# A hybrid decoder layer on one core: where the split weight operands lie in on-chip memory

## The chip, the core and the metric

The kernel runs on one core of one Trainium2 chip. The core has a matrix engine (TensorE, "PE" in the profile, with its weight loads as "PEld"), VectorE ("DVE"), ScalarE ("ACT"), GpSimd ("POOL") and SyncE ("SP"), whose queue issues most transfers. On-chip memory (SBUF) has 128 partitions; a tile takes the same range of bytes in each of them. The results of matmuls go to PSUM. The metric is the device time of one execution, in microseconds.

## The reference, cut to what matters

```python
def swiglu(u, w_in, w_out):
    gate, up = jnp.split(u @ w_in, 2, axis=-1)
    return (jax.nn.silu(gate) * up) @ w_out
...
        f1 = swiglu(rms_norm(h, ffn1_pre_g[l]), ffn1_w_in[l], ffn1_w_out[l])
        h = h + HALF_STEP * rms_norm(f1, ffn1_post_g[l])
        u = rms_norm(h, mix_pre_g[l])
        p_rwkv, p_swa, q_mem, gate_logits = _split(u @ w_in[l], IN_SIZES)
        y_a = rwkv7_mix(p_rwkv, ...)
        y_b = sliding_window_gqa_sinks(q_s, k_s, v_s, swa_sinks[l])
        y_c = memory_cross_attention(...)
        g_a, g_b, g_c = _split(jax.nn.sigmoid(gate_logits + gate_b[l]), (D, D, D))
        merged = (g_a * (y_a @ w_branch[l, 0]) + g_b * (y_b @ w_branch[l, 1])
                  + g_c * (y_c @ w_branch[l, 2]))
        h = h + rms_norm(merged @ w_out[l], mix_post_g[l])
        f2 = swiglu(rms_norm(h, ffn2_pre_g[l]), ffn2_w_in[l], ffn2_w_out[l])
        h = h + HALF_STEP * rms_norm(f2, ffn2_post_g[l])
```

There are 1024 tokens, a model width of 1024, an FFN width of 2816 and one layer; everything is float32. Nearly all of the arithmetic is in the products with the large weights: `w_in` and `w_out` of the two FFNs, `w_in` of the mixer, `w_branch` and `w_out`.

## The kernel before

Activations lie feature by feature: a tile has 128 features in the partitions and 512 tokens in the free dimension, and the tokens are worked in two halves of 512.

**A product in three matmuls.** A large product is made with float32 operands that are split in two float32r parts each: `hi` is the value rounded to float32r, `lo` is what is left. `mm3` (L314 to L319) then issues three matmuls into the same PSUM tile: `hi` weights with `hi` activations (L317), `hi` weights with `lo` activations (L318), and `lo` weights with `hi` activations (L319). Each matmul has 128 x 128 weights and 512 columns of the moving operand (256 in parts of the last stage), and each one loads its weights anew, the same `hi` block twice included. The weight load of a matmul runs while the matmul before it streams.

**How weights become operands.** A raw piece of weights, 128 partitions by four blocks of 128 columns (256 KB), is brought by SyncE's queue into one of five `w_raw` buffers (L246). `operand` (L251) makes `w_hi` from it with a ScalarE cast (L254) and `w_lo` with a VectorE subtraction (L256). Each side has eight buffers, which are used in turn (`OPS = 8`); `prefetch` keeps up to eight operands ahead of the matmuls. A cast therefore waits until the last matmul that reads the buffer's former content is done. For the FFN input products some sums and differences of raw weights are made first (L272 to L278, `w_sum`), and their results go through `operand` too. Eight operands of the last stage are kept in a pool of their own (`keep`), with tiles of the same names.

**Order.** The stages follow each other on TensorE: the first norm and the memory's keys and values; FFN 1 (input products, then output products in five chunks); the mixer's projections with the RWKV recurrence and the two attentions, between whose small matmuls the gates' projections are filled in; the branches and the output projection; FFN 2; and the last norm. The weights of all of them come through the same `operand` in one sequence, `self.seq`. Scheduling is left to a planner, with priorities around the casts (`high_priority`).

**Where the tiles lie.** All operand tiles, weights and activations, begin at a multiple of 32 bytes. A `w_hi` or `w_lo` tile is 4 x 128 numbers, 2048 bytes in each partition; block `k` is the contiguous piece of 512 bytes at `512 k`, and a matmul takes its weights from one such block: `tuple(t[:, k % 4] for t in w[k // 4])` (`block`) or `t[:, k]` (`product`).

Of the kernel before, what the change touches and what calls it, by code (L numbers as in the profile page):

```python
# [11 lines left out]
F32R = mybir.dt.float32r  # L12
# [5 lines left out]
P = 128  # L18
# [15 lines left out]
NPAIR = 4  # L34
MAIN_PSUM = ("po", "px", "py", "pr", "pgate", "pq", "pb", "pw")
OPS = 8
KEEP = 4
RAWS = 5
KH = KD // 2
# [161 lines left out]
class Builder:  # L201
# [4 lines left out]
    def plan(self):  # L206
        seq = []
        for f in ("ffn1", "ffn2"):
            items = [(f + "_gate", j) for j in range(FIRST[f])] + [(f + "_rest", j) for j in range(FIRST[f])]
            items += [(f + "_pair", j) for j in range(FIRST[f], KF)]  # L210
            items += [(f + "_out", q) for c in OUT_STRIPS for q in c]

            items += [(f + "_out", q) for q in OUT_STRIPS[-1]] * (f == "ffn1")
            if f == "ffn1":
                seq += items
                first = [("win", f) for f in MIX_FIRST]
                seq += first + [("win", f) for f in FILL] + first
                seq += [("win", f) for p in range(NPAIR) for f in (8 + p, 4 + p, p) if f not in MIX_FIRST]
                seq += [("win", j) for j in ATT_BLOCKS]
                seq += [("win", 24 + g) for g in range(24)]  # L220
                seq += [("wb", 4 * i + q) for i in BRANCHES + BRANCHES[2:] for q in range(4)]
                seq += [("wout", o) for o in range(KD)] * 2
            else:
                seq += items
        self.seq = seq
        self.raws = []
        for name, i in seq:
            f, _, kind = name.partition("_")
            if kind in ("gate", "rest", "pair"):
                self.raws += [(f + "_in", i)] + [(f + "_in", i + KF)] * (kind != "gate")  # L230
            else:
                self.raws.append((name, i))
        self.raw_pos, self.raw_ready = 0, []
        self.lead, self.urgent = 300, 1000
        self.op_base = self.op_use = self.op_pos = 0
        self.ops_ready = []
        self.gen = self.operands()

    def raw(self, ahead):
# [8 lines left out]
            self.raw_pos += 1  # L248
        return self.raw_ready.pop(0)

    def operand(self, x, pool=None):  # L251
        pool = pool or self.wpool
        hi = pool.tile([P, 4, P], F32R, tag="w_hi", name="w_hi", bufs=OPS)
        self.nc.scalar.copy(hi, x)  # L254
        lo = pool.tile([P, 4, P], F32R, tag="w_lo", name="w_lo", bufs=OPS)
        self.nc.vector.tensor_tensor(lo, x, hi.bitcast(F32), ALU.subtract)  # L256
        return hi, lo

    def operands(self):
        V = self.nc.vector  # L260
        for name, i in self.seq:
            kind = name.partition("_")[2]
            a1 = self.raw(RAWS - 1)
            a2 = self.raw(RAWS - 2)
            pool = self.keep if name == "ffn2_out" and i in OUT_STRIPS[-1][:KEEP] else None
            if kind != "rest":
# [14 lines left out]

    def prefetch(self, n=OPS, lead=None):
        with self.tc.high_priority(offset=self.lead if lead is None else lead):
            while self.op_pos < self.op_base + n:
                o = next(self.gen, None)
                if o is None:
                    return
                self.ops_ready.append(o)
                self.op_pos += 1
# [1066 lines left out]
    def build(self):  # L1356
        nc, tc, io = self.nc, self.tc, self.io
        with contextlib.ExitStack() as outer, tc.tile_pool(reuse_waits="tile", name="consts", bufs=1) as cp, \
# [44 lines left out]
            with quarters() as self.qpool:  # L1403
# [16 lines left out]
                with tc.tile_pool(reuse_waits="tile", name="ffn_out", bufs=2) as pool, \  # L1420
                     tc.tile_pool(reuse_waits="tile", name="keep", bufs=OPS) as self.keep:
                    acc = self.acc_tiles()
# [78 lines left out]
```

## Time and profile before

| | |
|---|---|
| median of the runs | 2378.95 us (2 runs, 2378.08 to 2379.82) |
| the profiled execution | 2381.53 us |
| its span, first to last instruction | 2379.8 us |
| mean granted TensorE clock | 0.996 |
| instructions | 33514 |
| moved by DMA | 323.80 MB, 136 GB/s over the span |

The profile is of one execution. "Busy" is the time in which an engine works on at least one instruction; matmuls are pipelined, so that the record of one matmul overlaps with the next, and their number times their duration is more than the busy time. In rows of groups the numbers behind the bar are busy us and the mean ns of one instruction, and behind the second bar the idle time before them with what ended it. In rows of the timeline the two numbers are the start and the duration in us; rows that follow each other on one engine without a gap may be merged, with their count behind an x.

### The profile page before, as it was taken

How to read it: one execution, taken by the hardware profiler on the slowest of the kernel's cores; microseconds unless marked ns; L12 is line 12 of the kernel's file. 1: busy time of each engine (PE TensorE's matmuls, PEld its weight loads, DVE VectorE, ACT ScalarE, POOL GpSimd, SP SyncE). 2: the span in 40 equal slices, each digit the busy share in tenths (PEclk: the TensorE clock that was granted, in tenths of full speed). 3: DMA queues.
4: the chain of work that ended last, by engine and by line, in shares of the span. 5: the costliest groups of instructions: out<-in, count | busy, mean ns of one | idle time of the engine just before them, and what ended most of it. 6: DMA issues, size and time to landing. Idle time of an engine off the chain costs nothing.

```text
span 2379.8 us, 33514 instructions
## 1 busy us (share of the span) xinstructions
PE 2343.9 (98%) x12388; PEld 1916.1 (81%) x12388; DVE 1543.4 (65%) x2584; ACT 891.6 (37%) x1648; POOL 95.5 (4%) x134
## 2 busy tenths in 40 slices
PE   8999999999999999999999999999999999999998
PEld 6788888888888777888868887778888888878888
DVE  6986555655478776894655456475998765564535
ACT  5423333422345444223454455234652233342211
POOL 0000000000000000001310000240000000000000
PEclk9999999999999999999999999999999999999999
DMA  7453222533244325325444324555545432263303
GB/s 277 136 188 121 86 87 80 178 115 106 97 161 142 110 99 189 135 93 175 144 156 153 123 97 150 185 188 166 174 162 183 156 120 82 83 202 100 114 23 107
DMA packets 196195, 323.80 MB, mean 136 GB/s; under 512 B 35360, under 2 KB 65568, under 8 KB 195776
## 3 DMA queue, kind: packets, MB, share of 16 engines
q1 hardware_dynamic: 180000, 294.33, 37.7%
q10 hardware_dynamic: 16032, 27.33, 3.4%
q8 instruction: 98, 1.61, 0.3%
q14 instruction: 65, 0.53, 0.1%
HBM read 231.41 MB, written 89.13 MB: 135 GB/s over the span
## 4 chain that ended last, share of the span: by engine, by line
PE 89%; DVE 5%; DMA 3%; ACT 2%; issue 1%; ACTq 0%; SPq 0%; DVEq 0%
PE po L317 7%; PE po L318 6%; PE po L319 6%; PE px L317 6%; PE px L318 6%; PE px L319 6%; PE pgate L317 4%; PE pgate L319 4%; PE pgate L318 4%; PE pz L317 3%; PE pz L318 3%; PE pz L319 3%; PE pr L319 2%; PE pr L317 2%; PE pr L318 2%; PE pb L318 2%
## 5 line engine op out<-in xcount | busy, mean ns | idle before, releaser
L254 ACT CAST w_hi<-w_raw 128x512 fp32r<-128x512 f32 x544 | 336.6, 621 | 903.0 <-PE po L318 213.1
L256 DVE TENSOR_TENSOR w_lo<-w_raw,w_hi 128x512 fp32r<-128x512 f32 x544 | 381.5, 702 | 183.0 <-ACT w_hi L254 171.7
L317 PE MATMUL po<-u,w_hi 128*128 128x512 f32 (+1 forms) x768 | 285.9, 372 | 0.9 <-DVE acc L627 0.9
L318 PE MATMUL po<-u,w_hi 128*128 128x512 f32 (+1 forms) x768 | 285.3, 372 | 0.0
L319 PE MATMUL po<-u,w_lo 128*128 128x512 f32 (+1 forms) x768 | 285.3, 372 | 0.0
L630 DVE TENSOR_TENSOR acc<-po,acc 128x512 f32<-128x512 f32 (+1 forms) x136 | 89.6, 658 | 162.6 <-PE po L319 162.0
L317 PEld LDWEIGHTS po<-u,w_hi 128*128 128x128 f32 x768 | 144.7, 188 | 26.3 <-DVE acc L627 1.6
L318 PEld LDWEIGHTS po<-u,w_hi 128*128 128x128 f32 x768 | 144.7, 188 | 24.9
L319 PEld LDWEIGHTS po<-u,w_lo 128*128 128x128 f32 x768 | 144.7, 188 | 25.0
L317 PE MATMUL pgate<-u,w_hi 128*128 128x512 f32 x384 | 152.8, 398 | 0.0
L319 PE MATMUL pgate<-u,w_lo 128*128 128x512 f32 x384 | 151.8, 395 | 0.0
L318 PE MATMUL pgate<-u,w_hi 128*128 128x512 f32 x384 | 150.0, 391 | 0.0
L317 PE MATMUL px<-f,w_hi 128*128 128x512 f32 x352 | 137.6, 391 | 3.1 <-ACT u L543 0.9
L317 PE MATMUL px<-u,w_hi 128*128 128x512 f32 x352 | 137.3, 390 | 1.2 <-ACT vm L1110 0.9
L318 PE MATMUL pz<-u,w_hi 128*128 128x512 f32 x352 | 137.2, 390 | 0.2 <-DVE u L380 0.2
L319 PE MATMUL px<-u,w_lo 128*128 128x512 f32 x352 | 137.2, 390 | 0.0
L317 PE MATMUL pz<-u,w_hi 128*128 128x512 f32 x352 | 137.0, 390 | 0.1
L319 PE MATMUL pz<-u,w_lo 128*128 128x512 f32 x352 | 137.0, 389 | 0.0
L318 PE MATMUL px<-u,w_hi 128*128 128x512 f32 x352 | 137.0, 389 | 0.0
L318 PE MATMUL px<-f,w_hi 128*128 128x512 f32 x352 | 136.9, 389 | 0.0
L319 PE MATMUL px<-f,w_lo 128*128 128x512 f32 x352 | 136.9, 389 | 0.0
L389 ACT ACTIVATE sq<-acc 128x512 f32<-128x512 f32 (+1 forms) x104 | 61.0, 598 | 93.2 <-DVE acc L630 75.7
(314 smaller groups left out, 4665.7 us busy)
## 6 DMA issues: line engine op xcount, KB each, us to landing
w_raw<-in_ffn_in SPq DMA_DIRECT2D x220, 256.0 KB
w_raw<-in_win SPq DMA_DIRECT2D x112, 256.0 KB
w_raw<-in_ffn_out SPq DMA_DIRECT2D x104, 256.0 KB
hid_d<-g SPq DMA_DIRECT2D x88, 256.0 KB
hid<-hid_d SPq DMA_DIRECT2D x88, 256.0 KB
gate_d<-gate SPq DMA_DIRECT2D x24, 512.0 KB
pk_d<-pk ACTq DMA_DIRECT2D x4, 2560.0 KB
f<-pk_d SPq DMA_DIRECT2D x16, 640.0 KB
```

What stands on the lines that cost most here:

```text
L254: self.nc.scalar.copy(hi, x)
L256: self.nc.vector.tensor_tensor(lo, x, hi.bitcast(F32), ALU.subtract)
L317: mm(out, wh, xh, start=first, stop=False, **kw)
L318: mm(out, wh, xl, start=False, stop=False, **kw)
L319: mm(out, wl, xh, start=False, stop=last, **kw)
L389: nc.scalar.activation(sq, x, ACT.Square)
L630: self.nc.vector.tensor_tensor(out, ps, out, ALU.add)
```

## The change

The eight `w_hi` and eight `w_lo` buffers of the main pool become sixteen buffers with names and places of their own. A place is given by three numbers: `pad`, by how many numbers (4 bytes each) its tile is longer than 512; `start`, at which of them the operand begins; and `stride`. With stride 1 the four blocks lie one behind the other as before, only moved by `4 * start` bytes. With stride 4 they are interleaved by column: column `c` of block `k` lies at number `4 c + k`, so that a matmul's 128 weights lie 16 bytes apart. Operands of the `keep` pool stay as they were. The order in which buffers are used (0 to 7, then 0 again), the cast, the subtraction and the matmuls are the same; they get other addresses and steps.

```diff
+PLACES = {
+    "hi": [(8, 1, 1)] + [(8, 4, 1)] * 7,
+    "lo": [(0, 0, 4), (8, 2, 1), (0, 0, 4), (8, 7, 1), (0, 0, 4), (8, 1, 1), (0, 0, 4), (8, 7, 1)],
+}
...
+        self.place = 0
...
+    def operand_place(self, t, pad, start, stride):
+
+        x = self.wpool.tile([P, 4 * P + pad], F32R, tag=f"w_{t}{self.place}", name=f"w_{t}", bufs=1)[:, start : start + 4 * P]
+        if stride == 1:
+            return x.rearrange("p (k c) -> p k c", c=P)
+        return x.rearrange("p (c k) -> p k c", c=P)
+
     def operand(self, x, pool=None):
-        pool = pool or self.wpool
-        hi = pool.tile([P, 4, P], F32R, tag="w_hi", name="w_hi", bufs=OPS)
+        if pool:
+            hi, lo = (pool.tile([P, 4, P], F32R, tag="w_" + t, name="w_" + t, bufs=OPS) for t in ("hi", "lo"))
+        else:
+            hi, lo = (self.operand_place(t, *PLACES[t][self.place]) for t in ("hi", "lo"))
+            self.place = (self.place + 1) % OPS
         self.nc.scalar.copy(hi, x)
-        lo = pool.tile([P, 4, P], F32R, tag="w_lo", name="w_lo", bufs=OPS)
         self.nc.vector.tensor_tensor(lo, x, hi.bitcast(F32), ALU.subtract)
         return hi, lo
```

## The prediction

> **What bounds the kernel now.** I read the page first: the busy times, the granted clock and the chain of waits.
>
> ```profile
> span 2379.8 us, 33514 instructions
> ...
> PE 2343.9 (98%) x12388; PEld 1916.1 (81%) x12388; DVE 1543.4 (65%) x2584; ACT 891.6 (37%) x1648; POOL 95.5 (4%) x134
> ...
> PEclk9999999999999999999999999999999999999999
> ...
> PE 89%; DVE 5%; DMA 3%; ACT 2%; issue 1%; ACTq 0%; SPq 0%; DVEq 0%
> ```
>
> TensorE is busy for all but 36 us of the span, its clock is granted throughout, and 89% of the chain that ends last runs through it. So no wait is left that is worth much. The stretches say the same stage by stage (columns: length, then busy us and count of PE, PEld, DVE, ACT, POOL, then clock, DMA share, GB/s):
>
> ```profile
> 64.00:667.00 603.00, 599.95 (x2639) 493.39 (x2638) 373.07 (x595) 205.48 (x348) 3.30 (x12) 1.00 0.36 119
> 1010.00:1075.00 65.00, 65.00 (x289) 53.83 (x288) 63.45 (x70) 15.56 (x25) 0.00 (x0) 1.00 0.27 94
> 1735.00:2326.00 591.00, 589.36 (x2628) 487.90 (x2627) 370.33 (x584) 192.90 (x326) 0.00 (x0) 1.00 0.37 121
> ```
>
> The two FFN stages are half of the time; VectorE is at 62% in them and DMA at 0.37. Only 1010 to 1075 has a second engine near its limit. Time can go or come only through the time of one matmul, so I asked for the three lines of `mm3`, whose weights are `w_hi`, `w_hi` and `w_lo` (answers for L317, L318 and L319, in this order):
>
> ```profile
> 0.00:2380.00 2380.00, 1194.27 (x3088) 580.24 (x3088) 1.00 0.41 136
> 0.00:2380.00 2380.00, 1189.19 (x3088) 580.31 (x3088) 1.00 0.41 136
> 0.00:2380.00 2380.00, 1193.72 (x3088) 580.43 (x3088) 1.00 0.41 136
> ```
>
> That is 3 x 3088 = 9264 of the 12388 matmuls, each with its own weight load. Durations overlap, so what counts is the distance from start to start. The timeline of PE alone:
>
> ```profile
> 1509.27 0.40 PE L318 MATMUL pb<-u,w_hi 128*128 128x512 f32 x1
> ...
> 1510.43 0.39 PE L317 MATMUL pb<-u,w_hi 128*128 128x512 f32 x1
> ...
> 1550.63 0.39 PE L319 MATMUL pb<-u,w_lo 128*128 128x512 f32 x1
> ...
> 1556.07 0.39 PE L319 MATMUL pb<-u,w_lo 128*128 128x512 f32 x1
> ...
> 2344.74 0.28 PE L318 MATMUL po<-u,w_hi 128*128 128x256 f32 x1
> ...
> 2345.58 0.28 PE L319 MATMUL po<-u,w_lo 128*128 128x256 f32 x1
> ```
>
> From 1550.63 to 1556.07 lie 24 steps: 226.7 ns each. From 2344.74 to 2345.58 lie 7 steps of half the width: 120 ns. The difference, 106.7 ns for 256 columns, is 0.417 ns a column, so 512 columns stream in 213.3 ns and **13.3 ns a matmul are left over, whatever the width**. Is that simply the price of changing weights? Matmuls on plain fp32 answer it:
>
> ```profile
> 35.45 3.60 PE L1023 MATMUL pq<-mkv,mem_g 128*128 128x512 f32 x8
> L1023 PE MATMUL pq<-mkv,mem_g 128*128 128x512 f32 x32 | 14.1, 595 | 0.0
> 1379.75 1.69 PE L89 MATMUL ptr<-ident,sc 128*128 128x128 f32 x14
> L89 PE MATMUL ptr<-ident,sc 128*128 128x128 f32 x120 | 15.0, 276 | 0.1
> ```
>
> Without the last one's own duration, 8 of 512 columns take (3.60 - 0.595)/7 = 429 ns each and 14 of 128 columns (1.69 - 0.276)/13 = 109 ns each: 0.834 ns a column, and about 2 ns left over. They also change weights every time. They stream at half the speed, and pay 2 ns where `mm3` pays 13.3. So some 11 ns arise only where the moving operand is read at full speed while the next weights are read. Moreover the remainder is not constant: from 1509.27 to 1510.43, just after a wait, five steps take 232 ns each, and only then does the stream settle on 226.7. I read this as two readers in step: their relation in time decides how often one holds up the other. Every matmul reads both operands from tiles that start on the 32-byte grid, so the relation is the same each time.
>
> **The change part by part.** It adds no instruction, transfer, semaphore or queue entry, and moves none: still one cast and one subtraction an operand, still eight places on each side, each freed by the same last matmul. What changes is where the weights lie.
>
> *Weights off the grid.* All `w_hi` (2 of 3 loads) start 4 or 16 bytes off, and odd `w_lo` places (half of the third) 4, 8 or 28 bytes. That is 5/6 of 9264 = 7720 loads. Their price cannot be read in the trace of before, where no fp32r operand is off the grid, so bounds: at best 2 ns are left over as in the fp32 rows (-11.3 ns a load); at worst the 232 ns of the settling rows (+5.3 ns). I take 80% of 11 ns, 8.8 ns, nearer to the fp32 rows, because they show that weights can be changed and loaded at no more than 2 ns when the readers don't meet. 7720 x 8.8 ns = 68 us. Without the 11 ns on any load it would be 9264 x 11 = 102 us.
>
> *Even `w_lo` places interleaved.* 1544 loads (a sixth) step 16 bytes from column to column instead of 4. The load has room:
>
> ```profile
> L318 PEld LDWEIGHTS po<-u,w_hi 128*128 128x128 f32 x768 | 144.7, 188 | 24.9
> ```
>
> A record lasts 188 ns, but the 128-column rows above show loads following each other at 109 ns. Under a 512-column stream a load may take 213 ns, about twice that, before it shows. Bounds: -11 ns as above; +100 ns if it took three times 109 ns. I take 0, since neither reading at this step nor a load twice as long would show on TensorE.
>
> *The writes.* ScalarE writes `w_hi` off the grid, VectorE writes half of the `w_lo` at a 16-byte step:
>
> ```profile
> L254 ACT CAST w_hi<-w_raw 128x512 fp32r<-128x512 f32 x544 | 336.6, 621 | 903.0 <-PE po L318 213.1
> L256 DVE TENSOR_TENSOR w_lo<-w_raw,w_hi 128x512 fp32r<-128x512 f32 x544 | 381.5, 702 | 183.0 <-ACT w_hi L254 171.7
> ```
>
> No row has such a write; between unchanged and doubled (+0.7 us), some 290 of them (half of 588 less the 8 kept elsewhere) add 0 to 204 us to VectorE, from 65% to at most 73% of the span. Eight operands are prepared ahead, each good for 12 to 24 matmuls (2.7 to 5.4 us), and most of ScalarE's idle time before a cast ends when TensorE frees a place. That hides it; without that cover each interleaved write could hold TensorE by its 0.7 us. Where the cover is thin, 1010 to 1075, 289 matmuls use 12 operands, 6 of them interleaved: at most 4 us. I take 0.
>
> *Sum.* 89% of the chain and 98% of the span are TensorE's; I let 95% of the 68 us through, 65 us. The profiled execution took 2381.5 us in all (span 2379.8 and 1.7 around it): 2381.5 - 65 = 2316.5. The median shown, 2378.95, lies 2.6 lower, so 2314.
>
> **The rivals.** *A smaller share.* The same mechanism, with under 5 ns saved a load: 2331 to 2375, say 2350. For it: the settling rows show remainders that change with the relation and yet none near 2 ns.
>
> *No effect.* If all loads are shifted alike, the stream may settle into the same step, since it settles from different starts. Or the 11 ns are no meeting of reads at all but a fixed cost of fp32r. Then 2379. For it: 13.3 ns at both widths. Against it: a fixed cost would not have given 232. [...]
>
> *The step is lost.* With three weights at three offsets the stream may never settle and stay at the 232 ns of the settling rows: 5.3 ns x 9264 = +49 us, 2428.
>
> *The interleaved load is slow* (the rival on the slower side). Every column of it lies in a new 16 bytes. If that makes the load longer than the 213 ns it hides behind, each of the 1544 holds the next matmul; it decides from about twice 109 ns, and reaches 2% at (213 + 31)/109 = 2.2 times. At three times it costs 1544 x (327 - 213) = +176 us, less the 65: 2490; at two times nothing. Against it: the load must more than double before anything shows. [...]
>
> *VectorE binds*: at most the 4 us above in one stage, and it needs TensorE to gain nothing.
>
> **How the numbers follow.** Forecast 0.62 (its own range 2276 to 2331: all 102 us saved, or 2%); smaller share 0.10; no effect 0.10; step lost 0.06, which lies on the edge, half within 2% and half beyond; interleaved load slow 0.10; VectorE 0.02. The likeliest gives 2314. From 2270 (a little below the full saving, as the 2 ns may go too) to 2385 the first three cases are held, 0.82. Faster by over 2% (below 2331, about what a measurement of this kernel can tell from no change): 0.62. Within 2%: 0.10 + 0.10 + 0.03 + 0.02 = 0.25. Slower: 0.03 + 0.10 = 0.13.
>
> **What would show it.** Right: in long stretches the distance from start to start of `mm3` falls from 226.7 to about 218 ns, at half width from 120 to about 111, with the fp32 rows unchanged, and PE's count in an FFN stage fits in fewer us. By the weight that is loaded behind it, a matmul followed by an off-grid load should show the fall, one followed by an interleaved load not. Wrong: 226.7 again (no effect), 230 or more (step lost), or every sixth distance far longer than the rest (interleaved load). `w_lo` writes near 1.4 us with PE waiting on VectorE in 1010 to 1075 would show the writes' price. The forecast fails most easily in its 80%, which no row fixes.

## The result, and the profile after

The changed kernel takes 2442.48 us in the median of two runs (2440.93 to 2444.03), against 2378.95 before: the ratio is 1.0267, with a 95% interval of 1.0223 to 1.0311. It is slower by 63.5 us. The prediction said 2314, with a range from 2270 to 2385.

The page of the kernel after, with the lines that answer to those shown of before (`w_hi` is now cast in L270, `w_lo` made in L271, and the three matmuls of `mm3` are L332 to L334):

```profile
span 2439.1 us, 33504 instructions
...
PE 2402.9 (99%) x12388; PEld 1992.7 (82%) x12388; DVE 1639.5 (67%) x2584; ACT 892.2 (37%) x1648; POOL 98.4 (4%) x134
...
PE 84%; DVE 8%; DMA 3%; ACT 2%; issue 2%; POOL 0%; SPq 0%; ACTq 0%; DVEq 0%; POOLq 0%
...
L270 ACT CAST w_hi<-w_raw 128x512 fp32r<-128x512 f32 x544 | 336.6, 620 | 926.7 <-PE po L333 215.4
L271 DVE TENSOR_TENSOR w_lo<-w_raw,w_hi 128x512 fp32r<-128x512 f32 x544 | 487.5, 899 | 170.1 <-ACT w_hi L270 168.8
...
L334 PEld LDWEIGHTS po<-u,w_lo 128*128 128x128 f32 x768 | 185.4, 241 | 29.2
L333 PEld LDWEIGHTS po<-u,w_hi 128*128 128x128 f32 x768 | 144.2, 188 | 28.1
```

TensorE is busy 59.0 us longer (2343.9 to 2402.9) and the span grew by 59.3 us; its idle time is what it was (2379.8 - 2343.9 = 35.9 us before, 36.2 now). So the waits did not grow in total. The same number of matmuls took longer. Two costs of the interleave are plain: the weight loads of L334 last 241 ns in the mean instead of 188, and the `w_lo` writes 899 ns instead of 702. ScalarE's off-grid writes cost nothing (620 ns, 621 before).

How much one matmul takes is again read from the timeline of PE, in the middle of FFN 1, over 24 steps:

```profile
299.80 0.40 PE L333 MATMUL pz<-u,w_hi 128*128 128x512 f32 x1
...
305.41 0.39 PE L333 MATMUL px<-u,w_hi 128*128 128x512 f32 x1
...
2392.87 0.40 PE L334 MATMUL po<-u,w_lo 128*128 128x256 f32 x1
2393.11 0.28 PE L332 MATMUL po<-u,w_hi 128*128 128x256 f32 x1
2393.22 0.28 PE L333 MATMUL po<-u,w_hi 128*128 128x256 f32 x1
2393.34 0.28 PE L334 MATMUL po<-u,w_lo 128*128 128x256 f32 x1
2393.46 0.28 PE L332 MATMUL po<-u,w_hi 128*128 128x256 f32 x1
```

5.61 us for 24 matmuls are 233.8 ns each, where it was 226.7. Over the distances inside unbroken stretches of `mm3` at full width, some 8260 in each kernel, the mean went from 226.8 to 233.6 ns. (A distance of 300 ns or more holds a wait and ends a stretch; stretches of fewer than some 20 distances, and the first two distances of each, are left out.) 6.8 ns x 8880 matmuls of full width are 60 us, which is the whole loss. The rows near the end are at half width. The first matmul there has interleaved `lo` weights and is followed after 240 ns; the others, with plain weights, after 110 to 120 ns.

### The profile page after: what moved, and what is told of

Read it like the earlier page. It is cut to its first block, busy times and chain, and to the rows that moved or that the text cites. A ratio compares the mean times of both kernels' runs of the same rounds, so it can differ in the third digit from the quotient of the medians.

```text
span 2439.1 us, 33504 instructions
## 1 busy us (share of the span) xinstructions
PE 2402.9 (99%) x12388; PEld 1992.7 (82%) x12388; DVE 1639.5 (67%) x2584; ACT 892.2 (37%) x1648; POOL 98.4 (4%) x134
## 4 chain that ended last, share of the span: by engine, by line
PE 84%; DVE 8%; DMA 3%; ACT 2%; issue 2%; POOL 0%; SPq 0%; ACTq 0%; DVEq 0%; POOLq 0%
PE po L334 7%; PE po L333 7%; PE po L332 6%; PE px L332 6%; PE px L333 6%; PE px L334 6%; PE pgate L334 3%; PE pgate L332 3%; PE pgate L333 3%; PE pz L333 3%; PE pz L332 3%; PE pz L334 3%; DVE w_lo L271 2%; PE pr L334 2%; PE pr L333 2%
## 5 line engine op out<-in xcount | busy, mean ns | idle before, releaser
L270 ACT CAST w_hi<-w_raw 128x512 fp32r<-128x512 f32 x544 | 336.6, 620 | 926.7 <-PE po L333 215.4
L271 DVE TENSOR_TENSOR w_lo<-w_raw,w_hi 128x512 fp32r<-128x512 f32 x544 | 487.5, 899 | 170.1 <-ACT w_hi L270 168.8
L334 PE MATMUL po<-u,w_lo 128*128 128x512 f32 (+1 forms) x768 | 292.1, 380 | 0.0
L333 PE MATMUL po<-u,w_hi 128*128 128x512 f32 (+1 forms) x768 | 290.3, 378 | 0.0
L332 PE MATMUL po<-u,w_hi 128*128 128x512 f32 (+1 forms) x768 | 289.6, 377 | 0.6 <-DVE acc L642 0.6
L334 PEld LDWEIGHTS po<-u,w_lo 128*128 128x128 f32 x768 | 185.4, 241 | 29.2
L333 PEld LDWEIGHTS po<-u,w_hi 128*128 128x128 f32 x768 | 144.2, 188 | 28.1
L332 PEld LDWEIGHTS po<-u,w_hi 128*128 128x128 f32 x768 | 145.3, 189 | 16.3 <-DVE acc L642 1.1
L332 PE MATMUL pgate<-u,w_hi 128*128 128x512 f32 x384 | 154.9, 403 | 0.0
L334 PE MATMUL pgate<-u,w_lo 128*128 128x512 f32 x384 | 154.7, 403 | 0.0
L333 PE MATMUL pgate<-u,w_hi 128*128 128x512 f32 x384 | 153.0, 398 | 0.0
L332 PE MATMUL px<-f,w_hi 128*128 128x512 f32 x352 | 139.7, 398 | 3.1 <-DVE up L569 2.3
L333 PE MATMUL pz<-u,w_hi 128*128 128x512 f32 x352 | 140.2, 398 | 0.3 <-DVE u L395 0.2
L332 PE MATMUL px<-u,w_hi 128*128 128x512 f32 x352 | 139.7, 397 | 0.4 <-ACT w_hi L270 0.4
L333 PE MATMUL px<-u,w_hi 128*128 128x512 f32 x352 | 139.8, 397 | 0.0
L333 PE MATMUL px<-f,w_hi 128*128 128x512 f32 x352 | 139.7, 397 | 0.0
L334 PE MATMUL px<-u,w_lo 128*128 128x512 f32 x352 | 139.4, 396 | 0.0
L332 PE MATMUL pz<-u,w_hi 128*128 128x512 f32 x352 | 139.3, 396 | 0.0
L334 PE MATMUL px<-f,w_lo 128*128 128x512 f32 x352 | 138.8, 394 | 0.0
L334 PE MATMUL pz<-u,w_lo 128*128 128x512 f32 x352 | 138.8, 394 | 0.0
L334 PEld LDWEIGHTS pgate<-u,w_lo 128*128 128x128 f32 x384 | 95.6, 249 | 17.3 <-issue 0.5
```

The costliest lines, as they stand in the source:

```text
L332: mm(out, wh, xh, start=first, stop=False, **kw)
L333: mm(out, wh, xl, start=False, stop=False, **kw)
L334: mm(out, wl, xh, start=False, stop=last, **kw)
```

## The experiments

All kernels keep the sixteen named places of the change and differ in the table of places, except where the edit says more. Times are one execution each, beside one of the kernel before on the same chip; "distance" is the mean from start to start of full-width `mm3` matmuls in unbroken stretches, as above. The kernel before took 2376.53 to 2382.57 us in these runs, so differences of a few us between two kernels decide nothing.

| kernel | us | before, same chip | difference | distance, ns |
|---|---|---|---|---|
| before | - | 2378.95 | - | 226.8 |
| after | 2442.48 | 2378.95 | +63.5 | 233.6 |
| tiles longer, all on the 32-byte grid | 2418.13 | 2379.02 | +39.1 | 232.5 |
| interleave only | 2426.66 | 2379.02 | +47.6 | 230.2 |
| offsets only | 2414.93 | 2379.02 | +35.9 | 232.2 |
| all 16 bytes off, tiles longer | 2414.47 | 2379.02 | +35.5 | 232.0 |
| names only | 2381.44 | 2380.03 | +1.4 | 226.8 |
| all weights 32 bytes on | 2423.22 | 2380.03 | +43.2 | 233.2 |
| seven places, 256 bytes longer | 2391.38 | 2380.03 | +11.4 | 226.8 |
| the same, all 16 bytes off | 2430.68 | 2380.03 | +50.7 | 232.6 |
| interleave, writing half | 2400.90 | 2377.80 | +23.1 | 226.9 |
| interleave, reading half | 2406.90 | 2377.80 | +29.1 | 230.2 |
| weights and activations 32 bytes on | 2383.91 | 2376.53 | +7.4 | 226.8 |

### First group: taking the change apart

The first theory was the prediction's own fourth case, the lost step: the stream of matmuls settles on 226.7 ns only while every load stands in the same relation to the moving operand. Its rivals were the long interleaved load, and a cost of its own for every weight off the 32-byte grid. The first kernel was meant as a control.

**Longer tiles, everything on the 32-byte grid.**

```diff
-    "hi": [(8, 1, 1)] + [(8, 4, 1)] * 7,
-    "lo": [(0, 0, 4), (8, 2, 1), (0, 0, 4), (8, 7, 1), (0, 0, 4), (8, 1, 1), (0, 0, 4), (8, 7, 1)],
+    "hi": [(8, 0, 1)] * 8,
+    "lo": [(8, 0, 1)] * 8,
```

> Sixteen buffers with places of their own as in the change, tiles 32 bytes longer, but every operand starts on the 32-byte grid and no block is interleaved: what is left of the change is names, lengths and addresses. Settled-step theory (the stream settles on 226.7 ns a matmul only while every weight load stands in the same relation to the moving operand), long-load theory (the interleaved loads hold TensorE) and off-grid theory (every weight off the grid costs by itself) all expect the time of before, 2379 us within 5, and 226.7 ns from start to start. If the sixteen buffers themselves cost, it is nearer to 2440 us.

It took 2418.13 us, 39 more than before, with nothing off the grid and nothing interleaved. All three theories were wrong about it. Its page and 24 steps of its timeline:

```profile
span 2416.3 us, 33504 instructions
...
PE 2385.7 (99%) x12388; PEld 1917.0 (79%) x12388; DVE 1543.7 (64%) x2584; ACT 892.5 (37%) x1648; POOL 96.0 (4%) x134
```

```profile
299.63 0.40 PE L334 MATMUL px<-f,w_lo 128*128 128x512 f32 x1
...
305.21 0.39 PE L334 MATMUL py<-r,w_lo 128*128 128x512 f32 x1
```

5.58 us for 24: 232.5 ns. VectorE and the loads are as before; only TensorE is busy longer, by 41.8 us, of which 5.3 us come out of its idle time (30.6 us left). The distances alone, 5.7 ns x 8880, would be 50 us; some 11 us of them do not reach the time. Where TensorE waited before, a slower one waits less: the distances of 300 ns and more, for one, fall from 50.8 to 44.0 us in total.

**The interleave alone.**

```diff
+    "hi": [(0, 0, 1)] * 8,
+    "lo": [(0, 0, 4), (0, 0, 1)] * 4,
```

> Only the even w_lo places are interleaved; everything else lies on the grid as before. Long-load theory: all of the loss is here, about 2440 us, with the excess at the interleaved loads. Settled-step theory: a sixth of the loads differ from the rest, so the step is lost too, 2410 to 2440 us, with 230 ns or more at matmuls of all three lines, those behind plain loads too. Off-grid theory: 2379 to 2390 us.

2426.66 us and 230.2 ns. The distances under which an interleaved block is loaded are longer, as both the first and the second theory said: in the input products of the FFNs 231.0, 231.7, 234.9 and 235.7 ns in the mean for the four blocks of an operand. The distance from L332 to L333, under which a plain `w_hi` block is loaded, is longer too, 232.9 ns where the `w_lo` block of the same product is interleaved and 228.7 where it is not. Only the first theory said so, though its 230 ns at all three lines is not reached: L334 is followed after 228.4 ns in the mean. And 3.4 ns x 8880 are 30 us of the 47.6, so something else is in it.

**The offsets alone.**

```diff
+    "hi": [(8, 1, 1)] + [(8, 4, 1)] * 7,
+    "lo": [(0, 0, 1), (8, 2, 1), (0, 0, 1), (8, 7, 1), (0, 0, 1), (8, 1, 1), (0, 0, 1), (8, 7, 1)],
```

> The offsets of the change without the interleave: w_hi 4 or 16 bytes off the grid, odd w_lo places 8, 28, 4 and 28 bytes off, even w_lo places on the grid and plain. Settled-step theory: three weights at three offsets, the step is lost, 2420 to 2440 us and 230 to 234 ns. Off-grid theory: 5/6 of the loss, about 2430 us. Long-load theory: 2379 us or less, 226.7 ns.

2414.93 us, below all the slower expectations, and 232.2 ns. The long-load theory is out as the whole cause. This kernel is no slower than the one with longer tiles on the grid.

**All sixteen places 16 bytes off.**

```diff
+    "hi": [(8, 4, 1)] * 8,
+    "lo": [(8, 4, 1)] * 8,
```

> All sixteen places start 16 bytes off the grid, none is interleaved: off the grid, but every load in the same relation to the moving operand. Settled-step theory: 2379 us within 5, the stream settles on 226.7 ns or another constant step. Off-grid theory: slower than the offsets alone with every load off, about 2440 us. Long-load theory: 2379 us.

2414.47 us, the same again. Off-grid theory expected it to be the slowest. On the grid, off it by mixed amounts, off it by 16 bytes: three times +35.5 to +39.1 us. What these three share is the longer tile. A tile of 2080 bytes instead of 2048 moves every tile behind it by 32 bytes more. In the kernel before, by the addresses in the built program, all weight tiles and all activation tiles start 224 bytes past a multiple of 256, so that in all 9264 matmuls of `mm3` weights and moving operand agree modulo 256; with longer tiles on the grid the weights start at every multiple of 32 in turn, and 1784 of the 9264 agree. In the kernel after only 2 do. That became the new theory: the stream's step hangs on the relation modulo something larger than 32 bytes.

### Second group: the relation modulo 256

**Names only.** Sixteen places, but tiles of the old length.

```diff
+    "hi": [(0, 0, 1)] * 8,
+    "lo": [(0, 0, 1)] * 8,
```

> Sixteen buffers with places of their own, but no longer tiles: every weight tile starts 224 bytes past a multiple of 256, as the activations do. Longer-tile theory (the 32 bytes added to a tile move the next tiles against the activations by 32 more bytes each, so the relation changes from place to place and the stream does not settle): 2379 us within 5 and 226.7 ns from start to start. Sixteen-buffer theory (the other order and names cost): about 2418 us, as with the on-grid tiles.

2381.44 us and 226.8 ns: sixteen buffers, their order and names cost nothing. The 32 bytes do.

**All weights 32 bytes further on**, alike, behind a small tile of their own.

```diff
             self.plan()
+            nc.vector.memset(self.wpool.tile([P, 8], F32, name="w_shift"), 0.0)
```

> As names only, with 32 bytes put ahead of all weight tiles: all of them lie 32 bytes off the activations' 256-byte grid, all alike. If the stream settles whenever the relation is the same for every load: one constant distance, 226.7 ns or another, 2360 to 2400 us. If it settles only where weights and activations agree modulo 256: 230 to 233 ns changing from matmul to matmul, about 2415 us.

2423.22 us. Two dozen steps of its timeline:

```profile
299.76 0.40 PE L334 MATMUL px<-f,w_lo 128*128 128x512 f32 x1
...
305.36 0.40 PE L334 MATMUL py<-r,w_lo 128*128 128x512 f32 x1
```

5.60 us, 233.3 ns. Every load stands in the same relation, and it is slow all the same. So the stream does not need the same relation everywhere; it needs a good one. It does repeat itself: nearly all distances are a turn of 235 and 232 ns, with a 231 at every third turn. The step is not lost, it is another step.

**Seven places, tiles 256 bytes longer**, the second one with every operand 16 bytes off. `OPS` is 7 in both, which makes room for the longer tiles.

```diff
-OPS = 8
+OPS = 7
...
+    "hi": [(64, 0, 1)] * 7,
+    "lo": [(64, 0, 1)] * 7,
...
+    "hi": [(64, 4, 1)] * 7,
+    "lo": [(64, 4, 1)] * 7,
```

> Seven places a side with tiles 256 bytes longer, all starting on the activations' 256-byte grid: a control that keeps the relation with longer tiles. Longer-tile theory: length as such is harmless, 2379 us within 10 (one place less ahead may add some us), 226.7 ns. If longer tiles cost by themselves: about 2418 us.

> As the seven-place control, every operand 16 bytes off the grid, the same for all. If the same relation everywhere is what counts: a constant distance, within 2360 to 2400 us. If being off the grid costs by itself: above the seven-place control by 20 us or more, with a constant distance above 226.7 ns. If the forecast's idea holds that off-grid weights meet the moving operand less often: below the control.

The first took 2391.38 us at 226.8 ns: length as such leaves the distance alone. The 11.4 us that it is slower arise nearly all after 2320 us, in the last stage; the place less is the likely cause, but no kernel tests it by itself. The second took 2430.68 us, 39 more than its control. Its timeline shows something that no theory had: with the same start everywhere, it goes at two speeds.

```profile
103.24 0.39 PE L334 MATMUL pz<-u,w_lo 128*128 128x512 f32 x1
...
108.68 0.62 PE L334 MATMUL pz<-u,w_lo 128*128 128x512 f32 x2
...
119.83 0.40 PE L334 MATMUL pz<-u,w_lo 128*128 128x512 f32 x1
...
125.43 0.39 PE L334 MATMUL px<-u,w_lo 128*128 128x512 f32 x1
```

24 steps from 103.24 to 108.68 are 226.7 ns each, 24 steps from 119.83 to 125.43 are 233.3 ns. At 16 bytes both steps can be kept. Which one a stretch takes changes from wait to wait, and it is mostly the slow one: of 8283 distances only 965 are 226 or 227 ns long.

### Third group: which relation is good

**A scan.** Seven long places; the start, the same for both sides, changes every 24 operands.

```diff
+STARTS = [(0, 0), (8, 8), (16, 16), (24, 24), (32, 32), (40, 40), (48, 48), (56, 56), (1, 1), (2, 2), (3, 3), (4, 4), (5, 5), (6, 6), (7, 7), (0, 0), (12, 12), (20, 20), (28, 28), (36, 36), (44, 44), (52, 52), (60, 60), (64, 64)]
+PER = 24
...
+            starts = STARTS[self.made // PER % len(STARTS)]
+            self.made += 1
+            hi, lo = (self.operand_place(t, PLACES[t][0], s, PLACES[t][1]) for t, s in zip(("hi", "lo"), starts))
```

> One kernel that measures: seven places a side with tiles 256 bytes longer, and the start of the operands, the same for w_hi and w_lo, steps every 24 operands through 0, 32, 64, 96, 128, 160, 192, 224, 4, 8, 12, 16, 20, 24, 28, 0, 48, 80, 112, 144, 176, 208, 240 and 256 bytes past the activations' 256-byte grid. If the stream settles only where weights and activations agree modulo 256: 226.7 ns at 0 and 256 alone, 230 to 235 ns at all others. If modulo 64 or 128: 226.7 ns at those multiples too. If it is the 32-byte grid: 226.7 ns at every multiple of 32, which the shift of all tiles by 32 bytes already speaks against. If some other start is faster than 226.7 ns, a kernel that beats both is possible, as the forecast hoped; the time of the whole is 2391 to 2430 us either way.

The whole took 2418.11 us (before: 2382.57). The mean distance for each start in bytes past the activations' multiple of 256, over some 200 to 1100 full-width matmuls each that had twelve of the same start before them:

```
bytes off:    0     4     8    12    16    20    24    28    32    48    64    80
ns:       226.8 232.4 230.7 231.9 226.7 233.3 230.8 233.9 233.3 233.3 233.3 232.1
bytes off:   96   112   128   144   160   176   192   208   224   240
ns:       234.3 233.3 232.4 233.3 233.3 230.0 229.1 231.8 233.3 227.7
```

It is not the 32-byte grid: 32, 64 and 128 are as slow as 4 or 12. At 0 (and 256, counted with it) and at 16 the distance is 226.7 to 226.8, at 240 it is 227.7, elsewhere 229 to 234 ns. So agreement modulo 256 is good, as the first case expected, but it is not alone: 16 bytes kept the fast step throughout in this kernel.

**A second scan**, with one side at 0 and the other one moved (only the table differs).

```diff
+STARTS = [(0, 1), (0, 2), (0, 3), (0, 4), (0, 5), (0, 6), (0, 7), (0, 8), (0, 16), (0, 24), (0, 32), (0, 48), (1, 0), (2, 0), (3, 0), (4, 0), (5, 0), (6, 0), (7, 0), (8, 0), (16, 0), (24, 0), (32, 0), (48, 0)]
```

> Second measuring kernel, as the first, with one side on the 256-byte grid and the other off it: w_lo 4, 8, 12, 16, 20, 24, 28, 32, 64, 96, 128 and 192 bytes off while w_hi is at 0, then the same for w_hi while w_lo is at 0, 24 operands each. If all loads must agree with the activations for the stream to settle on 226.7 ns, all 24 give 229 to 235 ns. If the two loads of w_hi decide, w_lo may be off at 226.7 ns. If mixed starts avoid meetings, as the change intends by the forecast, some pair lies below 226.7 ns; none below means that no table of this kind can beat the kernel before.

2415.45 us (before: 2377.80).

```
bytes off:           4     8    12    16    20    24    28    32    64    96   128   192
w_lo off, hi at 0: 233.4 231.1 226.7 226.7 231.1 230.4 228.2 233.3 230.9 232.5 231.1 231.1
w_hi off, lo at 0: 231.1 231.2 229.4 232.0 233.3 230.6 232.2 231.9 233.3 230.0 233.3 228.9
```

Two of 24 pairs keep 226.7 ns, none goes below. Over both scans, 226.7 is the floor that was found, and the kernel before already stands on it; no table of plain offsets that was tried here beats it.

### Fourth group: the two halves of the interleave

In both kernels all tiles keep their place modulo 256. A block of an interleaved tile does not: block `k` starts `4 k` bytes into the tile. In the first kernel, the subtraction writes the even places at a 16-byte step and the matmuls read contiguous blocks, so the `lo` part of the product uses permuted weights; in the second it is the other way round, with the same consequence.

```diff
-        if stride == 1:
-            return x.rearrange("p (k c) -> p k c", c=P)
-        return x.rearrange("p (c k) -> p k c", c=P)
+        plain = x.rearrange("p (k c) -> p k c", c=P)
+        return plain, plain if stride == 1 else x.rearrange("p (c k) -> p k c", c=P)
...
-        self.nc.vector.tensor_tensor(lo, x, hi.bitcast(F32), ALU.subtract)
+        self.nc.vector.tensor_tensor(written, x, hi.bitcast(F32), ALU.subtract)
```

> The interleave alone, its writing half: VectorE writes the even w_lo places at a 16-byte step, but the matmuls read contiguous blocks, so their lo weights are permuted and that part of the product is not the reference's. Read theory (the 16-byte step makes the weight load longer and takes the stream out of its settled step): 2379 to 2390 us, 226.7 ns. Write theory (VectorE's 1.1 us writes hold TensorE or disturb its reads): 2400 us or more.

> The interleave alone, its reading half: VectorE writes all w_lo contiguously at its old speed, but the matmuls read the even places at a 16-byte step, so that part of the product is not the reference's. Read theory: 2410 to 2427 us, 231 to 236 ns at the matmuls behind which an interleaved block is loaded. Write theory: 2379 to 2390 us.

Neither theory was right alone: writing costs 23.1 us, reading 29.1 (2406.90 us, a little under what the read theory expected), together 52 where both halves cost 47.6. The page of the writing half first, then that of the reading half (its `w_lo` matmuls are L335):

```profile
span 2399.2 us, 33504 instructions
...
PE 2349.4 (98%) x12388; PEld 1915.0 (80%) x12388; DVE 1635.9 (68%) x2584; ACT 892.5 (37%) x1648; POOL 99.2 (4%) x134
...
PE 54%; DVE 7%; DMA 3%; ACT 2%; issue 1%; POOL 1%; ACTq 0%; SPq 0%; DVEq 0%; POOLq 0%
```

```profile
span 2405.2 us, 33504 instructions
...
PE 2373.5 (99%) x12388; PEld 1989.0 (83%) x12388; DVE 1543.2 (64%) x2584; ACT 893.2 (37%) x1648; POOL 96.0 (4%) x134
...
L335 PEld LDWEIGHTS po<-u,w_lo 128*128 128x128 f32 x768 | 185.2, 241 | 27.4
```

In the writing half the distance is unchanged and TensorE is busy only 5.5 us longer, but idle for 49.8 us instead of 35.9: VectorE, 92 us busier, hands its results over later (the waits of `ps_ms` for VectorE's `sq`, for example, went from 4.0 to 7.7 us).

In the reading half VectorE is as before, TensorE's idle time is no longer than before (31.7 us), and its distance is 230.2 ns. Some 9 of the 29 us arise at the 1433 full-width distances under which an interleaved block is loaded (233.4 ns in the mean), some 3 in the part at half width, and most of the rest at distances under which plain weights are loaded. Two things are mixed in it, the 16-byte step and the starts 4, 8 and 12 bytes off. Block 0, which starts in agreement, separates them in part: in the input products of the FFNs the distance just before it, under a plain load, is still 226.7 ns, the one under which block 0 is loaded 231.0 ns. So the step by itself costs something; how much of the 234.9 and 235.7 ns of blocks 2 and 3 is due to their starts was not tested.

### Relation or address

Every kernel so far moved the weights and left the activations. The last one moves the activations by 32 bytes modulo 256 too.

```diff
+            nc.vector.memset(self.wpool.tile([P, 8], F32, name="w_shift"), 0.0)
+            shift = outer.enter_context(tc.tile_pool(reuse_waits="tile", name="shift", bufs=1, side="right"))
+            nc.vector.memset(shift.tile([P, 56], F32, name="u_shift"), 0.0)
```

> As the kernel in which all weights lie 32 bytes further on, but the activations are moved by 32 bytes modulo 256 as well (224 bytes put ahead on the other end of the memory). Relation theory (what counts is where the weights lie against the moving operand): the loss is gone, 2380 us within 5 and 226.7 ns. Address theory (the weights' own addresses count, 224 modulo 256 being a good one): as with the weights moved alone, about 2423 us and 233 ns.

2383.91 us, and the fast step is back:

```profile
299.82 0.39 PE L334 MATMUL px<-u,w_lo 128*128 128x512 f32 x1
...
305.26 0.39 PE L334 MATMUL px<-u,w_lo 128*128 128x512 f32 x1
```

5.44 us for 24 matmuls: 226.7 ns. With the weights at the very same addresses as in the kernel that took 2423 us (the same in all 9264 matmuls), the slow step is gone. What counts is the relation between weights and moving operand; a good value of it is agreement modulo 256, and the change leaves it. The 7.4 us by which this one execution is above the kernel before are not in the distance; they were not followed up.

## Why the prediction was wrong

**What bounds the kernel** was right. TensorE's busy time and the span grew by the same 59 us, its idle time did not grow, and the whole difference lies in the distance from one `mm3` matmul to the next.

**The step that failed is the term for weights off the grid**: "I take 80% of 11 ns, 8.8 ns, nearer to the fp32 rows, because they show that weights can be changed and loaded at no more than 2 ns when the readers don't meet." The fp32 rows show what is left over at half the streaming speed (0.834 ns a column against 0.417); they say nothing on whether moving the weights gets a full-speed stream there. The kernel with the offsets alone, its longer tiles included, costs 5.4 ns a matmul (226.8 to 232.2) instead of saving 8.8. The row that did bear on it was the other bound, the five settling steps at 232 ns: it was the one observation in the trace of a stream out of its settled step, and it was slower. (It was not another relation of addresses: by the built program weights and activations agree there too.) The trace showed that the stream settles on 226.7 from many starts; none of the rows showed it settle lower, and nor did any relation in the two scans.

**A part was left out of the sum.** I took the longer tiles as mere room for the offsets and took it that the 32-byte grid fixes the relation. It does not: weights and activations agreed modulo 256. Longer tiles move the next ones against the activations by multiples of 32, and that alone costs 39 us where the change costs 63.5. Offsets within the tile add nothing to it (35.9 and 35.5 us with them). A smaller slip: the eight operands of `keep` stay as they were, so that 1496 loads are interleaved and not 1544.

**The interleaved load** was taken at 0 because it hides behind a stream of 213 ns. That reading of the room was nearly right: the load's record went from 188 to 310 ns, at half width a matmul with such weights is followed after some 230 to 240 ns instead of 120, and at full width no distance is far longer than the rest. But I missed that such a load changes the stream's step for the matmuls around it too: reading alone costs 29 us (230.2 ns). The slow load as a rival, deciding from about twice its length, did not come as 2490 us: by the rows at half width the load about doubles, and at full width the distance with it is 233.4 ns, 6.6 above the settled one.

**The writes** at a 16-byte step take 1084 ns where plain ones take 684 (medians of some 290 `w_lo` writes of each kind in the kernel after), within the bounds given. I took 0, as the operands prepared ahead would hide them. Alone they cost 23.1 us, so the cover does not hold while TensorE runs at its fast step. Beside the slower reading (230.2 ns) they still cost some 18 us (47.6 - 29.1). Their share in the change itself (233.6 ns) was not measured by a kernel: TensorE's idle time is 36.2 us with them and 29.9 (2413.1 - 2383.2) in the kernel with the offsets alone, which speaks for a few us. That offsets and reading add up to 65 us (35.9 + 29.1), near the 63.5, is in part chance: their distances do not add (5.4 + 3.4 = 8.8 ns, measured 6.8).

**The rivals.** "The step is lost" named the right place and the right row and gave 2428; it had 0.06. Its cause, three weights at three offsets, is not needed: one common shift by 32 bytes does it. And there the stream does not stay unsettled; it settles into another repeating pattern (235 and 232 ns in turn, with a 231 at every third turn). That 2428 lies near 2442 is partly luck, as it holds nothing for the interleave. "No effect" held that a stream whose loads are all shifted alike settles into the same step, or that the remainder is a fixed cost of fp32r. 2423 us and 233.3 ns with all weights moved by 32 bytes, against 2384 us and 226.7 ns with the activations moved as well, decide against both for these fp32r matmuls of 512 columns. What a step of 16 bytes between neighbours costs the instruction itself no row of before could say; in the kernel after it is about 120 ns on the record of a load of 128 columns (188 to 310) and 400 ns on a write of 512 numbers (684 to 1084).

What stays open is why agreement modulo 256 is good: the runs show which relations keep the fast step, not the mechanism, and the two readers that hold each other up remain an interpretation. How the 63.5 us of the change divide between places, interleaved reading and writes is open as well; that the places alone cost 35 to 39 us and the reading alone 29 is measured.

## What to carry to other kernels

When a matmul stream runs at a steady distance with a remainder, compare that distance before and after any change that moves a tile, even a change of padding or of a buffer's length: here 32 bytes cost 1.6 to 1.8% through nothing but addresses. Keep weight tiles and moving tiles congruent (here modulo 256 bytes, most simply by tile sizes that are multiples of it: 226.7 ns a matmul in agreement, 233.3 with all weights 32 bytes on), and check an address idea with one kernel that scans many starts before building a table on it. Test costs both alone and together: writes that cost 23 us alone cost some 18 beside the slower reading.

## What was not expected of the hardware

- The distance between fp32r matmuls of 512 columns depends on where the weights lie against the moving operand modulo 256 bytes: 226.7 ns in agreement, 229 to 234 ns at most other places, with the same instructions on all engines.
- Some means turn up again and again: of the 22 starts of the first scan eight give 233.3 ns, one 230.0 and two 226.7 or 226.8, values 3.3 ns apart. The other eleven lie at none of them.
- At one and the same relation (16 bytes) two patterns hold, 226.7 and 233.3 ns, and after a wait the stream can be in the other one.
- A weight load whose columns lie 16 bytes apart has a record of 310 ns instead of 188, and a VectorE write at that step takes 1084 ns instead of 684 for 512 numbers a partition.
